# Down projection of a hybrid block: the last convolutions in steps, single PSUM banks for the second block, smaller tiles for the sums of weights

## Chip, cores and metric

The kernel runs on one core of a Trainium2 chip. The metric is the device time of one execution in microseconds; the median of three runs of the kernel before is 1498.23 us (1496.71 to 1498.31). The profile describes one execution, which itself took 1497.91 us. Engines: PE (TensorE, the matmuls), ACT (ScalarE), DVE (VectorE), POOL (GpSimd), SP (SyncE, here only a queue for DMAs).

## The reference

One layer of a transformer block in float32, 256 tokens of width 2048: three kinds of attention with gates, an output projection, and a feed-forward part. The change touches only the last:

```python
h2 = rms_norm(x, g_ffn[l])
u = causal_depthwise_conv(h2 @ w_up[l], conv_w[l], conv_b[l])   # 2048 -> 2 x 5632, three taps along the tokens
u_gate, u_val = jnp.split(u, 2, axis=-1)
x = x + (jax.nn.silu(u_gate) * u_val) @ w_down[l]               # 5632 -> 2048
```

## The kernel before

**Two parts of each number.** Every float32 operand of a matmul is split into a rounded part ("hi", a cast on ACT) and the rest ("lo", a subtraction on DVE), and a product is three matmuls: hi x hi, lo x hi and hi x lo. For the weights, a piece of 128 x 1024 is loaded into a "raw" buffer by SP (four buffers), cast on ACT into one of four hi buffers and subtracted on DVE into one of four lo buffers (`parts`, lines 886 and 887). A hi or lo buffer is free when the matmuls that read it four pieces ago are done.

**Up stage** (lines 791 to 813). The 44 tiles of 128 columns are taken in groups of four, once for the gate half (`s` = 0) and once for the value half (`s` = 1). A group has eight weight pieces and fills two PSUM pairs (a tile of two banks, `two_banks`). After the group `conv` is queued for each pair: it adds the two halves of the product, scales by the norm (`u`), applies three taps (activations on ACT at lines 739 and 743, adds on DVE at 744), and either applies Silu or multiplies by the gate and splits the product into hi and lo in `aT` (lines 750 to 753). `later` queues a generator, `tick` runs one step of each active one (at most `WINDOW` = 2); a `conv` is a generator without a yield, so that one tick issues all of it. Scratch tiles (`cr`, `z`) come from two shared buffers. During the up stage `weight_sums` also loads rows of the down weights into `r` (two buffers of 128 x 2 x 2 x 512) and adds them in place, lines 770 to 773; the sums go to DRAM for the "s" steps below.

**Down stage** (from line 818 on). It has two column blocks of 1024. A block's order is written out in `PLANS`: "e" is a plain product of two tiles of `aT` with two weight pieces, in two steps of 12 matmuls (the last one of a block does nothing in its first step and 24 in its second); "s" is a seven-product scheme in four steps (3, 6, 6 and 6 matmuls), which reads sums of `aT` tiles (`forms`, on DVE and ACT, lines 855 to 867) and the sums of weights. A block has four accumulators X and four Y, a bank each, held in four pair tiles. `gather` adds Y to the residual rows `xr` in three parts, one a tick, beginning three ticks after the last "s"; `finish` runs what is left of it at the block's end, and `results` then adds X (line 1017) and stores (line 1018). The second block begins with X on the pairs that held Y.

**What sets the order.** A list scheduler places the instructions, but `keep_in_program_order` (`keep`, `pin`) puts an instruction behind whatever was traced before it on its engine. All loads, casts and subtractions of the down stage are so pinned. Loads and casts of a step are issued two steps ahead of its matmuls (`AHEAD`). The convolutions of the last group are ticked after the first down step, so in program order they stand behind the casts of three pieces and ahead of the fourth; their own instructions are not pinned. Loads take a raw buffer, from the ninth on every third one a "more" buffer (`buffer`). `down_pool` closes the convolutions' pools and opens its own in their place.

## Time and profile before

| | |
|---|---|
| median of three runs | 1498.23 us |
| profiled execution | 1497.91 us, its span 1496.2 us |
| PE busy | 1482.3 us (99%) |
| DVE busy | 1043.6 us (70%) |
| ACT busy | 862.9 us (58%) |
| DMA | 327.70 MB, mean 219 GB/s |
| mean granted clock of PE | 0.997 |
| PE idle behind other engines, all waits | 7.9 us |
| longest of them | 4.3 us, once |

The span runs from the first to the last instruction. PE's busy time is modelled from the matmuls' starts. The up stage ends and the down stage begins at 1256.3 us, its second block at 1378.1 us, and the last matmul ends at 1490.4 us. Rows of a timeline give start, duration, engine, line, operation, what is written and read, and in brackets the engine's idle time ahead of it and what ended it.

### The profile page before, as it was taken

The numbers are of one execution on the slowest core, as the hardware profiler recorded it, in microseconds if no ns is written. First come the engines' busy times: TensorE is split into PE (matmuls) and PEld (weight loads), VectorE is DVE, ScalarE is ACT, GpSimd is POOL, SyncE is SP. The second block draws the span as 40 slices with busy tenths as digits, with TensorE's granted clock in tenths as the row PEclk, the third lists the DMA queues.
The fourth block names the chain that finished last, engine by engine and source line by source line (L and its number), as shares of the span: only waits on it lengthen the run. The fifth ranks groups of instructions, "written<-read, shape, count | busy, mean of one in ns | idle before, by whom it ended". The sixth has DMA issues, their size and how long they took to land.

```text
span 1496.2 us, 20140 instructions
## 1 busy us (share of the span) xinstructions
PE 1482.3 (99%) x7408; PEld 1250.7 (84%) x7408; DVE 1043.6 (70%) x1333; ACT 862.9 (58%) x1225; POOL 35.8 (2%) x81
## 2 busy tenths in 40 slices
PE   9999999999999999999999999999999998999998
PEld 6888888888888888888888888888888887888886
DVE  5766566555655646556557778778778776998987
ACT  6755454458544444444457667667667666655653
POOL 0000000001000000000000000000000000001000
PEclk9999999999999999999999999999999999999999
DMA  8675475475666677665676877877877774778874
GB/s 296 203 204 157 127 223 157 119 224 149 196 198 206 192 203 199 191 193 191 219 227 221 281 249 257 274 259 241 273 264 248 262 218 151 254 267 257 291 264 155
DMA packets 155921, 327.70 MB, mean 219 GB/s; under 512 B 11290, under 2 KB 20142, under 8 KB 155822
## 3 DMA queue, kind: packets, MB, share of 16 engines
q1 hardware_dynamic: 150798, 310.15, 66.3%
q0 software_dynamic: 4272, 15.21, 2.8%
q8 instruction: 58, 0.95, 0.3%
q10 hardware_dynamic: 752, 1.06, 0.2%
q14 instruction: 41, 0.34, 0.1%
HBM read 312.21 MB, written 14.16 MB: 218 GB/s over the span
## 4 chain that ended last, share of the span: by engine, by line
PE 96%; ACT 2%; DVE 1%; DMA 1%; issue 0%; POOL 0%; SPq 0%; DVEq 0%; POOLq 0%; ACTq 0%
PE u L805 22%; PE u L807 11%; PE g L158 5%; PE g L160 5%; PE g L159 5%; PE d L893 5%; PE d L891 5%; PE d L892 5%; PE s L158 2%; PE s L160 2%; PE f L158 2%; PE f L160 2%; PE s L159 2%; PE f L159 2%; PE b L160 2%; PE b L159 2%
## 5 line engine op out<-in xcount | busy, mean ns | idle before, releaser
L805 PE MATMUL u<-hT,hi_u 128*128 128x512 f32 x1408 | 442.4, 396 | 0.1
L807 PEld LDWEIGHTS u<-hT,lo_u 128*128 128x128 f32 x1408 | 264.5, 188 | 62.5
L807 PE MATMUL u<-hT,lo_u 128*128 128x256 f32 x1408 | 276.6, 278 | 0.0
L148 DVE TENSOR_TENSOR lo_u<-raw_u,hi_u 128x1024 fp32r<-128x1024 f32 x176 | 214.1, 1221 | 72.7 <-ACT hi_u L147 70.9
L147 ACT CAST hi_u<-raw_u 128x1024 fp32r<-128x1024 f32 x176 | 183.4, 1048 | 103.0 <-PE u L805 92.3
L805 PEld LDWEIGHTS u<-hT,hi_u 128*128 128x128 f32 x1408 | 214.4, 189 | 0.5 <-issue 0.5
L148 DVE TENSOR_TENSOR lo_g<-raw_g,hi_g 128x1024 fp32r<-128x1024 f32 x96 | 117.7, 1229 | 101.3 <-ACT hi_g L147 99.0
L147 ACT CAST hi_g<-raw_g 128x1024 fp32r<-128x1024 f32 x96 | 100.8, 1052 | 121.8 <-PE g L159 96.8
L158 PE MATMUL g<-hi_g,xT 128*128 128x512 f32 x384 | 150.9, 393 | 0.0
L160 PE MATMUL g<-lo_g,xT 128*128 128x512 f32 x384 | 149.6, 390 | 0.0
L159 PE MATMUL g<-hi_g,xT 128*128 128x512 f32 x384 | 149.5, 389 | 0.0
L160 PEld LDWEIGHTS g<-lo_g,xT 128*128 128x128 f32 x384 | 72.1, 188 | 15.3
L159 PEld LDWEIGHTS g<-hi_g,xT 128*128 128x128 f32 x384 | 72.2, 188 | 14.6
L158 PEld LDWEIGHTS g<-hi_g,xT 128*128 128x128 f32 x384 | 72.1, 188 | 14.5
L891 PE MATMUL d<-hi_d,aT 128*128 128x512 f32 x200 | 79.0, 395 | 4.3 <-ACT hi_d L886 4.3
L744 DVE TENSOR_TENSOR y<-y,z 128x512 f32<-128x512 f32 x88 | 60.8, 691 | 26.7 <-ACT z L743 22.9
L893 PE MATMUL d<-lo_d,aT 128*128 128x512 f32 x200 | 78.9, 395 | 0.0
L892 PE MATMUL d<-hi_d,aT 128*128 128x512 f32 x200 | 78.8, 394 | 0.0
L743 ACT ACTIVATE z<-u,taps 128x256 f32<-128x256 f32 x176 | 74.6, 496 | 0.0
L148 DVE TENSOR_TENSOR lo_s<-raw_s,hi_s 128x1024 fp32r<-128x1024 f32 (+1 forms) x40 | 44.7, 1118 | 37.2 <-ACT hi_s L147 37.1
L148 DVE TENSOR_TENSOR lo_f<-raw_f,hi_f 128x1024 fp32r<-128x1024 f32 (+1 forms) x40 | 44.7, 1120 | 34.5 <-ACT hi_f L147 33.0
L147 ACT CAST hi_f<-raw_f 128x1024 fp32r<-128x1024 f32 (+1 forms) x40 | 38.6, 967 | 52.3 <-PE f L159 47.6
(324 smaller groups left out, 2796.6 us busy)
## 6 DMA issues: line engine op xcount, KB each, us to landing
raw_u<-in_w_up_dram SPq DMA_DIRECT2D x176, 512.0 KB, 4.7
raw_g<-in_w_in_dram SPq DMA_DIRECT2D x96, 512.0 KB, 3.8
raw_d<-in_w_down_dram SPq DMA_DIRECT2D x50, 512.0 KB, 5.4
r<-in_w_down_dram SPq DMA_DIRECT2D x76, 256.0 KB, 5.6
raw_s<-in_w_down_dram SPq DMA_DIRECT2D x38, 512.0 KB, 5.2
raw_f<-in_w_in_dram SPq DMA_DIRECT2D x32, 512.0 KB, 3.6
raw_s<-in_w_in_dram SPq DMA_DIRECT2D x32, 512.0 KB, 3.6
raw_o<-in_w_out_dram SPq DMA_DIRECT2D x32, 512.0 KB, 5.0
```

Of the source, the lines that this page charges most:

```text
L147: pin(nc.scalar.copy(hi[:, :m], raw[:, :m]))
L148: pin(nc.vector.tensor_tensor(lo[:, :m], raw[:, :m], hi[:, :m].bitcast(F32), ALU.subtract))
L158: nc.tensor.matmul(o, lhsT=xh, rhs=wh, start=first, stop=False)
L159: nc.tensor.matmul(o, lhsT=xl, rhs=wh, start=False, stop=False)
L160: nc.tensor.matmul(o, lhsT=xh, rhs=wl, start=False, stop=last)
L743: nc.scalar.activation(z[:, i], u[:, i, j : j + S], AF.Copy, scale=taps_of(j, i))
L744: nc.vector.tensor_tensor(y, y, z, ALU.add)
L805: nc.tensor.matmul(ps, lhsT=hi[:, j, c], rhs=hT[:, k + j, :], start=first, stop=False)
L807: nc.tensor.matmul(ps[:, :S], lhsT=lo[:, j, c], rhs=hT[:, k + j, :S], start=False, stop=last)
L891: nc.tensor.matmul(o, lhsT=ah, rhs=w[0], start=first, stop=False)
L892: nc.tensor.matmul(o, lhsT=al, rhs=w[0], start=False, stop=False)
L893: nc.tensor.matmul(o, lhsT=ah, rhs=w[1], start=False, stop=last)
```

## The change

- `conv` of the last group's value half (`tail`: tiles 40 and 42) yields five times, so that it takes six ticks: scaled product; first two activations with the middle tap; last tap; product with the gate; hi part; lo part. There are now two `u` tiles that take turns. `tick` lets four generators be active in the down stage.
- `PLANS`: the first block has five "e" before its first "s" and two after its last "s" (before: four and three). Its forms begin with the fourth "e" instead of the second. "More" buffers are used from the twelfth load on.
- The second block's accumulators are eight single-bank tiles of a new pool, opened when the pair pool closes. The list of tiles is turned by half, as the list of pairs was.
- `weight_sums` has the first row's halves in a tile `r0` with one buffer and the second row's in `r1` with two. The sums and their order are the same.

```diff
-PLANS = ("eeee" + "se" * 8 + "ee", "e" + "se" * 4 + "sse" + "se" * 3 + "ssee")
+PLANS = ("eeeee" + "se" * 7 + "see", "e" + "se" * 4 + "sse" + "se" * 3 + "ssee")
...
-    waiting, active = deque(), []
+    waiting, active, window = deque(), [], [WINDOW]
...
-        while waiting and len(active) < WINDOW:
+        while waiting and len(active) < window[0]:
...
-    pp2.append(ctx.enter_context(tc.tile_pool(name="pp2", bufs=4, space=bass.MemoryType.PSUM, reuse_waits="tile")))
+    pp2x = ctx.enter_context(ExitStack())
+    pp2.append(pp2x.enter_context(tc.tile_pool(name="pp2", bufs=4, space=bass.MemoryType.PSUM, reuse_waits="tile")))
...
-        u = cp.tile([P, 2, S + 2], F32, tag="u", bufs=1, name="u")
-        nc.vector.memset(u[:, :, 0:2], 0.0)
-        cps.extend((cp, u, sp))
+        us = [cp.tile([P, 2, S + 2], F32, bufs=1, name=f"u{i}") for i in range(2)]
+        for u in us:
+            nc.vector.memset(u[:, :, 0:2], 0.0)
+        cps.extend((cp, us, sp))
...
     def conv(ps, f, s):
-        cp, u, _ = cps
+        cp, us, _ = cps
+        u = us[f // 2 % 2]
...
+        tail = f >= FT - 4 and s == 1
...
         nc.vector.tensor_tensor(u[:, :, 2:], cr, rbc.unsqueeze(1).to_broadcast([P, 2, S]), ALU.mult)
+        if tail:
+            yield
...
             nc.vector.tensor_tensor(y, y, z, ALU.add)
+            if tail:
+                yield
...
             nc.vector.tensor_tensor(g, g, y, ALU.mult)
+            if tail:
+                yield
             a = aT[:, f : f + 2]
             nc.scalar.copy(a[:, :, :S], g)
+            if tail:
+                yield
             nc.vector.tensor_tensor(a[:, :, S:], g, a[:, :, :S].bitcast(F32), ALU.subtract)
-        return
-        yield
-
+            ended.append(f)
...
-        r = cps[2].tile([P, 2, 2, 512], F32, tag="r", name=f"r_{nb}_{p}")
+        r = [
+            cps[2].tile([P, 2, 512], F32, tag=f"r{j}", bufs=1 + j, name=f"r{j}_{nb}_{p}") for j in range(2)
+        ]
         for j, n in ((0, 1), (0, 0), (1, 1), (1, 0)):
             tc.keep_in_program_order(
-                nc.sync.dma_start(r[:, j, n], dv[:, 2 * p + j, n0 + n * 512 : n0 + (n + 1) * 512])
+                nc.sync.dma_start(r[j][:, n], dv[:, 2 * p + j, n0 + n * 512 : n0 + (n + 1) * 512])
             )
...
-        b01 = r[:, 0, 1]
-        tc.keep_in_program_order(nc.vector.tensor_tensor(r[:, 0, 0], r[:, 0, 0], b01, ALU.add))
+        add = lambda o, i: tc.keep_in_program_order(nc.vector.tensor_tensor(o, o, i, ALU.add))
+        add(r[0][:, 0], r[0][:, 1])
         yield 1
-        tc.keep_in_program_order(nc.vector.tensor_tensor(r[:, 1, 1], r[:, 1, 1], r[:, 0, 0], ALU.add))
-        tc.keep_in_program_order(nc.vector.tensor_tensor(r[:, 1, 0], r[:, 1, 0], r[:, 1, 1], ALU.add))
+        add(r[1][:, 1], r[0][:, 0])
+        add(r[1][:, 0], r[1][:, 1])
...
-        if turn[0] > 8 and turn[0] % 3 == 0:
+        if turn[0] > 10 and turn[0] % 3 == 0:
...
     def start(nb):
-        b = [two_banks(f"d{nb}_{i}") for i in range(4)]
-        if nb:
-            b = b[2:] + b[:2]
-        X = [[b[t][:, n] for n in range(2)] for t in range(NT)]
-        Y = [b[2 + i // 2][:, i % 2] for i in range(4)]
-        banks[nb] = X, Y
+        if nb == 0:
+            pairs = [two_banks(f"d{nb}_{i}") for i in range(4)]
+            b = [pair[:, i] for pair in pairs for i in range(2)]
+        else:
+            pp2x.close()
+            pp3 = ctx.enter_context(tc.tile_pool(name="pp3", bufs=8, space=bass.MemoryType.PSUM, reuse_waits="tile"))
+            b = [pp3.tile([P, 512], F32, tag="bank", name=f"d{nb}_{i}") for i in range(8)]
+            b = b[4:] + b[:4]
+        banks[nb] = [[b[2 * t + n] for n in range(2)] for t in range(NT)], b[4:]
...
-                if formed < ns and n_done >= 2:
+                if formed < ns and n_done >= 4 - 2 * nb:
...
+    window[0] = 4
     for f in after_step.pop(-1):
         f()
```

More of the change, by code (lines that the diff above doesn't have):

```diff
@@ L750, in conv @@
             nc.vector.tensor_tensor(g, g, y, ALU.mult)
+            if tail:
+                yield
             a = aT[:, f : f + 2]
             nc.scalar.copy(a[:, :, :S], g)
+            if tail:
+                yield
             nc.vector.tensor_tensor(a[:, :, S:], g, a[:, :, :S].bitcast(F32), ALU.subtract)
-        return
-        yield
+            ended.append(f)
+    ended = []
     made = {}
@@ L776, in weight_sums @@
         yield 2
-        nc.gpsimd.dma_start(T, r[:, 1].rearrange("p b n -> p (b n)"))
+        nc.gpsimd.dma_start(T, r[1].rearrange("p b n -> p (b n)"))
     adding = []
@@ L821, in down_pool @@
         if not dn:
+            assert len(cps) == 3 and len(ended) == FT // 2
             uv.close()
```

## The prediction

> **What bounds the kernel now.** The page's first part comes first: TensorE (PE) is busy for the whole span, so only time in which PE stands still or runs slowly can be won. The answer on PE's waits lists that time. Line 891 is the first matmul of a product in the down stage, and its one wait of 4.3 us is more than all others together.

> ```profile
> span 1496.2 us, 20140 instructions
> PE 1482.3 (99%) x7408; PEld 1250.7 (84%) x7408; DVE 1043.6 (70%) x1333; ACT 862.9 (58%) x1225; POOL 35.8 (2%) x81
> ...
> PE d L891 <- ACT hi_d L886: 4.3, 1, 4.3
> PE spare L102 <- DVE qscale L244: 1.2, 1, 1.2
> PE mT L195 <- DMA memres<-in_mem_dram: 1.2, 1, 1.2
> ```

> Next, the timeline of PE around that wait, and the sums by stretch (their columns: length, busy time of PE, PEld, DVE, ACT, POOL, then the granted clock, DMA share, GB/s).

> ```profile
> 1263.98 0.39 PE L892 MATMUL d<-hi_d,aT 128*128 128x512 f32 x1
> 1264.21 0.39 PE L893 MATMUL d<-lo_d,aT 128*128 128x512 f32 x1
> 1268.89 0.79 PE L891 MATMUL d<-hi_d,aT 128*128 128x512 f32 x1 [4.29 <-ACT hi_d L886]
> ...
> 1274.58 0.47 PE L891 MATMUL d<-hi_d,aT 128*128 128x512 f32 x1
> 1274.89 0.39 PE L892 MATMUL d<-hi_d,aT 128*128 128x512 f32 x1
> ...
> 1264.40:1268.90 4.50, 0.21 (x2) 0.01 (x1) 2.80 (x5) 3.02 (x7) 1.64 (x3) 0.89 0.27 95
> 1268.90:1274.60 5.70, 5.66 (x13) 3.97 (x14) 5.37 (x9) 3.57 (x6) 0.00 (x0) 0.50 0.71 213
> 1300.00:1320.00 20.00, 20.00 (x90) 16.57 (x89) 19.80 (x31) 12.74 (x16) 0.00 (x0) 1.00 0.75 260
> ```

> Matmuls normally start 0.227 us apart, so the one at 1268.89 was due at 1264.44: 4.45 us lost. After the pause the granted clock is 0.50 for 5.7 us. From 1268.89 to 1274.89 lie 13 starts, 6.00 us where 13 x 0.227 = 2.95 would do: 3.05 more. The stall is worth **7.5 us**, not 4.3.

> Its cause stands on ACT's timeline.

> ```profile
> 1253.45 1.05 ACT L886 CAST hi_d<-raw_d 128x1024 fp32r<-128x1024 f32 x1 [1.74 <-PE u L805]
> 1255.77 0.59 ACT L734 COPY cr<-u 128x512 f32<-128x512 f32 x1 [1.27 <-PE u L807]
> 1257.84 1.10 ACT L739 ACTIVATE y<-u,taps 128x256 f32<-128x256 f32 x2 [1.48 <-DVE u L736]
> 1258.84 1.70 ACT L743 ACTIVATE z<-u,taps 128x256 f32<-128x256 f32 x4
> 1260.55 0.59 ACT L734 COPY cr<-u 128x512 f32<-128x512 f32 x1
> 1262.49 0.62 ACT L752 CAST aT<-y 128x512 fp32r<-128x512 f32 x1 [1.36 <-DVE y L750]
> ...
> 1267.27 0.62 ACT L752 CAST aT<-y 128x512 fp32r<-128x512 f32 x1 [1.49 <-DVE y L750]
> 1267.80 2.94 ACT L886 CAST hi_d<-raw_d 128x1024 fp32r<-128x1024 f32 x3
> ```

> Three casts of down weights are done by 1254.5. Then come both last convolutions, one after the other, 12 us of which ACT spends 4.3 waiting for DVE; the fourth cast is pinned behind them and starts at 1267.80. PE has three steps of 12 x 0.227 = 2.72 us in hand from 1256.27 and runs dry at 1264.44.

> **The last convolutions in six steps.** No instruction is added; what each of the steps 0 to 5 puts ahead of the next cast changes. I walk the queues with the durations of the rows. ACT: both copies end at 1257.1, the fourth cast at 1258.1 (it needs the last up matmul's buffer, free at 1256.3). Then two activations and two scalings of each convolution, 2 x 1.9, to 1261.9; fifth cast to 1262.9; the other scalings, 2 x 0.85, to 1264.6; sixth cast to 1265.6. DVE: four operations of about 0.65 to 1259.1, the low part of the fourth piece to 1260.3; two adds, fifth low part to 1264.1; two adds, sixth to 1266.8; products, seventh to 1269.2. PE wants pieces four to seven at 1264.44, 1267.16, 1269.88 and 1272.60: each is 3 us early or more. Over the ten first steps (27.2 us, five "e" now) DVE has nine low parts (1.15 each), 12 operations of the convolutions (0.65) and two sets of forms (2.8): 23.8 us. So the stall goes, and with it the half clock: **-7.5**, with -4.45 as the poorer bound if some other short wait still costs the clock. The second u buffer is what lets the two convolutions overlap; earlier it changes nothing, since the two scratch buffers keep them in turn.

> **Plan and forms.** The matmuls are the same (8 "s" and 14 "e" in the first block). Forms start two "e" later, so six "se" pairs carry one instead of five. The row of 1300 to 1320 is such a stretch: DVE 19.80 of 20.00 us, and PE never waits. I cost it at 0; what hides it is PE's lead over DVE, and without that one more set of forms is 2.8 us late. Load nine goes to a raw buffer instead of a "more" one: it can start when piece five is read out, at 1264.1, 13.9 us before its step (1256.27 + 8 x 2.72): 0.

> **Sums of weights.** The first half now has one buffer, so its next load, which is on SP's queue, waits for the add at line 772 of the sum before, and the up weights queue behind it.

> ```profile
> 1175.51 0.42 SPq L765 DMA_DIRECT2D r<-in_w_down_dram  x1
> 1176.82 0.37 SPq L146 DMA_DIRECT2D raw_u<-in_w_up_dram  x1
> ...
> 1180.22 0.69 DVE L772 TENSOR_TENSOR r<-r 128x512 f32<-128x512 f32 x1
> ...
> 1183.83 1.05 ACT L147 CAST hi_u<-raw_u 128x1024 fp32r<-128x1024 f32 x1 [1.73 <-PE u L805]
> ...
> DMA to landing us min/median/max: 3.6/4.7/6.6
> ```

> The load slips from 1175.51 to 1180.91 and the up piece from 1176.82 to 1181.35. It lands 6.6 us later at worst (the last row, of raw_u), at 1188.0; cast 1.05 and low part 1.23 end at 1190.3. That piece is second in its group; the group's copies on ACT come each 22.29 us, PE needs it at 1256.27 - 3 x 22.29 + 2.79 = 1192.2. Cost **0**, with 1.9 us to spare.

> **Single banks at the end.** The DVE rows are the last sums of the first and the second block.

> ```profile
> 1378.26 1.29 DVE L1017 TENSOR_TENSOR xr<-xr,d 128x512 f32<-128x512 f32 x2 [1.35 <-PE d L893]
> ...
> 1487.74 1.28 DVE L1017 TENSOR_TENSOR xr<-xr,d 128x512 f32<-128x512 f32 x2
> 1490.46 1.35 DVE L1017 TENSOR_TENSOR xr<-xr,d 128x512 f32<-128x512 f32 x3 [1.43 <-PE d L893]
> 1488.46 4.05 ACTq L1018 DMA_DIRECT2D out_dram<-xr  x5
> GB/s 0 0 0 0 0 46 337 391 364 373 355 319 146 0 0 0 0 55 346 373 387 314 332 323 196 5 0 0 0 0 0 0 0 0 36 0 0 0 0 0
> ```

> The last row is the DMA rate in 40 slices from 1488 to 1497. The third sum has its matmuls complete 1.36 us (six matmuls) before the last, but waits for the whole pair; so three adds and three stores follow the last matmul. With banks of their own only two halves follow: the last store is issued at 1490.46 + 0.41 + 0.03 + 0.47 = 1491.4 instead of 1492.0. I take **-0.65**; the bounds are 0, if the stores are slow for another reason, and -1.35, if the 256 KB that no longer share the end also bring the landing forward (0.7 us at 373 GB/s).

> **Single banks at the boundary of the blocks.** Here the change can take back. Before, the second block's X (which its first step writes) takes the pairs that held Y. The new pool is a fresh one, and the reordering of the list by the code doesn't choose places: in the compiled kernel before, a fresh pool gives place 0 to the tile used first, then places from the top down (the pair pool: banks 0, 6, 4, 2). X of the first block lies in banks 0-1 and 6-7. The new X then gets 0, 7, 6 and 5: the second matmul triple of the block waits for the last of the four result adds. When is that? Only two "e" follow the last "s" now, so parts two and three of the gathering of Y come together in the last step.

> ```profile
> 1369.39 0.68 DVE L990 TENSOR_TENSOR f<-e,d 128x512 f32<-128x512 f32 x1
> 1371.31 1.22 DVE L887 TENSOR_TENSOR lo_d<-raw_d,hi_d 128x1024 fp32r<-128x1024 f32 x1
> 1372.44 0.68 DVE L994 TENSOR_TENSOR xr<-xr,e 128x512 f32<-128x512 f32 x1
> 1374.49 1.22 DVE L887 TENSOR_TENSOR lo_d<-raw_d,hi_d 128x1024 fp32r<-128x1024 f32 x1
> ...
> 1372.60 1.05 ACT L886 CAST hi_d<-raw_d 128x1024 fp32r<-128x1024 f32 x1 [1.66 <-PE d L892]
> ...
> 1378.06 0.39 PE L891 MATMUL d<-hi_d,aT 128*128 128x512 f32 x1
> 1378.74 0.39 PE L891 MATMUL d<-hi_d,aT 128*128 128x512 f32 x1
> ```

> In the old clock times: the cast ends at 1373.65, its low part at 1374.9; gathering 1.92 + 2.05 (the distances 1369.39 to 1371.31 and 1372.44 to 1374.49) to 1378.8; four adds to 1381.3. PE wants the first triple at 1378.06 (its adds end at 1380.1) and the second at 1378.74: it stands 2.05 us, runs 0.68, stands 0.55, and is **+2.6** late. Bounds: 0, if X gets Y's old banks (those are read out at 1378.2, before the third triple's turn at 1379.42), and 2.6 + 3.05 if the clock drops too. Behind the waiting matmul stands all of PE; the casts behind it only gain lead.

> On whether 2.05 us lowers the clock there is a row from the start:

> ```profile
> 12.63 0.44 PE L195 MATMUL mT<-ident,memres 128*128 128x128 f32 x2 [1.17 <-DMA memres<-in_mem_dram]
> ...
> 12.00:14.00 2.00, 1.37 (x7) 1.19 (x8) 1.83 (x3) 1.38 (x3) 0.00 (x0) 1.00 0.73 268
> ```

> 1.17 us of idling left 1.00, 4.29 us gave 0.50; 2.05 is nearer the first. [...]

> **Sum**, against the profiled execution (1497.91 us, span 1496.2): -7.5 - 0.65 + 2.6 = -5.55, a span of 1490.65. The median of the runs is 0.32 above the profiled one; from 1498.23 the forecast is **1492.7**.

> **Rivals.**
> 1. The boundary costs nothing (X lands on Y's old banks, or the scheduler finds other matmuls): -8.15, **1490.1**. For it: before, no wait stands at the boundary. Against it: the order of places.
> 2. The boundary's pauses lower the clock: +3.05, **1495.7**. Against it stands the 1.17 us row; for it, two pauses close together.
> 3. The change doesn't do what it says: the convolutions' pieces are not themselves pinned, and if they still stand in one run ahead of the fourth cast, the 7.5 us stay: **1500.2**. Against it: every cast is pinned behind whatever was traced before it.
> 4. Slower by SP: the single buffer of the sums. The place is the second piece of 18 groups; it decides from a landing of 8.5 us (6.6 + 1.9), and each further 0.5 us costs 18 x 0.5 = 9: **1501.7**. Against it: 6.6 is the slowest landing seen.

> **How the numbers follow.** Forecast 0.50, rival 1 0.27, rival 2 0.10, rival 3 0.07, rival 4 0.03, anything else (the extra forms' 2.8 us, 1495.5, among it) 0.03. The range must hold the forecast, rival 1 with its end at the better bound (1490.1 - 0.7 = 1489.4) and rival 2 (1495.7): 1489.4 to 1496.0. A measurement of this kernel tells about 0.2% (3 us) from no change, so faster means under 1495.2: forecast, rival 1 and a third of rival 2, 0.80; same 0.10; slower 0.10.

> **What would show it.** Right: no wait of line 891 on the casts near 1264, granted clock 1.00 there; the copies of line 734 both ahead of the fourth cast, the scalings after it; a PE wait on the sums of line 1017 near 1371 (1378 less 7.5), about 2.6 us in all with the clock at 1.00; after the last matmul two adds and two stores. Wrong: that wait absent (rival 1), a clock under 1 behind it (rival 2), PE waits on up casts (rival 4), or any wait of PE on low parts between steps 10 and 40, which would mean that DVE could not carry the moved forms.

## The result, and the profile after

The changed kernel takes **1492.72 us** (median of six runs, 1491.44 to 1494.12). The kernel before, in six runs beside it, takes 1498.06 us (1496.71 to 1498.36). The ratio is 0.9964, with a 95% interval of 0.9954 to 0.9974: faster, by about 0.36%. The profiled execution is the slowest of the six, 1494.12 us.

Page of the changed kernel, first part:

```profile
span 1492.4 us, 20170 instructions
...
PE 1483.2 (99%) x7408; PEld 1252.3 (84%) x7408; DVE 1043.4 (70%) x1334; ACT 862.4 (58%) x1225; POOL 35.6 (2%) x81
```

PE's waits in the changed kernel (total, times, longest). Line 906 is the first matmul of a product (891 before), line 1035 the addition of the results (1017 before):

```profile
PE d L906 <- DVE xr L1035: 2.2, 2, 2.0
PE spare L102 <- DVE qscale L244: 1.2, 1, 1.2
```

The wait of 4.3 us on a cast is gone. A new one has come, twice, 2.2 us in all, on the results of the first block.

**Where the stall went.** ACT's timeline in the changed kernel, from the last casts of the up stage on (start, duration, instruction):

```profile
1254.45 1.05 ACT L901 CAST hi_d<-raw_d 128x1024 fp32r<-128x1024 f32 x1 [1.74 <-PE u L819]
1256.77 1.28 ACT L738 COPY cr<-u 128x512 f32<-128x512 f32 x2 [1.27 <-PE u L821]
1257.95 1.05 ACT L901 CAST hi_d<-raw_d 128x1024 fp32r<-128x1024 f32 x1
1259.41 1.10 ACT L745 ACTIVATE y<-u,taps 128x256 f32<-128x256 f32 x2 [0.41 <-DVE u L740]
...
1263.00 1.03 ACT L901 CAST hi_d<-raw_d 128x1024 fp32r<-128x1024 f32 x1
1263.94 1.70 ACT L749 ACTIVATE z<-u,taps 128x256 f32<-128x256 f32 x4
1265.55 1.98 ACT L901 CAST hi_d<-raw_d 128x1024 fp32r<-128x1024 f32 x2
```

Both copies now stand together and the fourth cast right behind them, at 1257.95 where it was at 1267.80. The convolutions' scalings fill the gaps between the casts. (In this execution the down stage begins 1.0 us later than in the one before, at 1257.27; so 1.0 us is to be taken off when times are set side by side.)

**Where the new wait is.** PE at the boundary of the two blocks, and below it DVE over the same time:

```profile
1371.29 0.39 PE L908 MATMUL d<-lo_d,aT 128*128 128x512 f32 x1
1373.67 0.47 PE L906 MATMUL d<-hi_d,aT 128*128 128x512 f32 x1 [1.99 <-DVE xr L1035]
...
1374.20 0.40 PE L908 MATMUL d<-lo_d,aT 128*128 128x512 f32 x1
1374.77 0.79 PE L906 MATMUL d<-hi_d,aT 128*128 128x512 f32 x1 [0.17 <-DVE xr L1035]
...
1378.30 0.40 PE L908 MATMUL d<-lo_d,aT 128*128 128x512 f32 x1
...
1371.63 0.69 DVE L1011 TENSOR_TENSOR xr<-xr,e 128x512 f32<-128x512 f32 x1
1372.24 2.47 DVE L1035 TENSOR_TENSOR xr<-xr,d 128x512 f32<-128x512 f32 x4
```

The four result additions end at 1374.71. The first triple of the second block starts at 1373.67 instead of 1371.52 (the start before it plus 0.227), and the second at 1374.77, right behind the fourth addition.

The sums by stretch of the changed kernel (length, busy time of PE, PEld, DVE, ACT, POOL, then granted clock, DMA share, GB/s):

```profile
1373.30:1374.80 1.50, 0.96 (x4) 0.52 (x4) 1.50 (x4) 0.00 (x0) 1.40 (x3) 1.00 0.33 126
1374.80:1376.50 1.70, 1.70 (x4) 1.42 (x5) 1.70 (x3) 0.00 (x0) 0.92 (x3) 0.50 0.91 313
1376.50:1378.30 1.80, 1.80 (x6) 1.38 (x6) 1.16 (x2) 0.00 (x0) 0.94 (x3) 0.52 0.85 228
1378.30:1380.00 1.70, 1.70 (x9) 1.41 (x8) 0.42 (x1) 1.05 (x1) 0.66 (x2) 1.00 1.27 128
1257.30:1285.00 27.70, 27.70 (x125) 22.93 (x124) 24.92 (x38) 18.48 (x31) 0.00 (x0) 1.00 0.63 203
```

The last row is the place of the old stall: PE busy for all of it, at full clock. The rows above it show that in this execution the new pauses are followed by 3.5 us at half clock. From 1374.77 to 1378.30 lie eight starts, 3.53 us where 8 x 0.227 = 1.82 would do: 1.7 us more.

**The end.** DVE's last additions and the issues of the stores in the changed kernel:

```profile
1486.86 0.69 DVE L1035 TENSOR_TENSOR xr<-xr,d 128x512 f32<-128x512 f32 x1 [0.23 <-PE d L908]
1488.22 0.75 DVE L1035 TENSOR_TENSOR xr<-xr,d 128x256 f32<-128x256 f32 x2 [0.67 <-PE d L908]
...
1486.07 3.43 ACTq L1036 DMA_DIRECT2D out_dram<-xr  x5
```

The third sum no longer waits for the last matmul (it starts at 1486.86, the matmuls end at 1488.18). Only two halves follow, and the last store is issued 0.87 us behind the last matmul, where it was 1.62 before.

The three stretches, from the traces: the down stage from its first matmul's start to its last one's end, and from there to the end of the span.

| | down stage | from its end to the span's end |
|---|---|---|
| before | 234.16 | 5.75 |
| changed | 230.91 | 4.23 |
| difference | -3.25 | -1.52 |

The sum is -4.8; the two profiled spans differ by 3.8, since this execution reached the down stage 1.0 us later.

### The profile page after: what moved, and what is told of

It is laid out like the page before. It is cut to its first block, busy times and chain, and to the rows that moved or that the text cites. A ratio compares the mean times of both kernels' runs of the same rounds, so it can differ in the third digit from the quotient of the medians.

```text
span 1492.4 us, 20170 instructions
## 1 busy us (share of the span) xinstructions
PE 1483.2 (99%) x7408; PEld 1252.3 (84%) x7408; DVE 1043.4 (70%) x1334; ACT 862.4 (58%) x1225; POOL 35.6 (2%) x81
## 3 DMA queue, kind: packets, MB, share of 16 engines
q0 software_dynamic: 4272, 15.21, 2.8%
## 5 line engine op out<-in xcount | busy, mean ns | idle before, releaser
L147 ACT CAST hi_u<-raw_u 128x1024 fp32r<-128x1024 f32 x176 | 182.8, 1048 | 109.8 <-PE u L819 78.4
L147 ACT CAST hi_g<-raw_g 128x1024 fp32r<-128x1024 f32 x96 | 100.8, 1052 | 121.8 <-PE g L159 97.2
L750 DVE TENSOR_TENSOR y<-y,z 128x512 f32<-128x512 f32 x88 | 60.6, 690 | 21.2 <-ACT z L749 17.6
L147 ACT CAST hi_f<-raw_f 128x1024 fp32r<-128x1024 f32 (+1 forms) x40 | 38.6, 967 | 52.5 <-PE f L159 47.6
```

What stands on the lines that cost most here:

```text
L147: pin(nc.scalar.copy(hi[:, :m], raw[:, :m]))
L750: nc.vector.tensor_tensor(y, y, z, ALU.add)
```

## Experiments

**Theory**: the change is three separate sums. The convolutions in steps win the whole stall, pause and half clock, about 7.5 us. The boundary gives back 2.7 us, since the fresh pool puts the second block's X on the banks that are read out last. The end wins somewhat more than a microsecond. **Rivals**: the boundary's wait comes from the later gathering (the moved "e"), whatever bank X has; the stall was won by the second u buffer, the moved "e" or the smaller sums, not by the steps; and the boundary's price is mostly the half clock, not the pauses.

| kernel | edit | median us (range, runs) | ratio to before (95%) |
|---|---|---|---|
| e0_again | the changed kernel | 1493.14 (1491.86 to 1493.96, 6) | 0.9969 (0.9956 to 0.9981) |
| e1_placed | X on the banks of the old Y | 1488.65 (1488.55 to 1489.80, 5) | 0.9941 (0.9928 to 0.9953) |
| e2_whole | last convolutions in one step | 1498.95 (1498.28 to 1501.51, 10) | 1.0011 (1.0002 to 1.0020) |
| e3_pairs | second block in pairs again | 1490.24 (1489.87 to 1491.04, 5) | 0.9950 (0.9938 to 0.9963) |
| e4_plan | plan of before | 1490.11 (1489.87 to 1491.18, 5) | 0.9951 (0.9938 to 0.9963) |
| e5_sums_only | before, with the smaller sums alone | 1498.06 (1496.81 to 1499.95, 11) | 1.0001 (0.9992 to 1.0010) |
| e6_long | two more additions ahead of the results | 1494.71 (1493.83 to 1495.73, 11) | 0.9980 (0.9971 to 0.9989) |
| e7_banks_only | before, with the single banks (and the smaller sums) | 1497.63 (1496.56 to 1499.16, 11) | 1.0001 (0.9992 to 1.0009) |

The first four ran beside a median of 1497.90 us for the kernel before, the others beside 1497.83. All but e6_long compute what the kernel computes in the same additions and products; e6_long adds two additions whose results nothing uses.

### e0_again: the same kernel once more

> The changed kernel once more, unaltered. Its profile showed two PE waits on the result adds at the block boundary (1.99 and 0.17 us) and then half clock for 3.5 us; its six times spread over 2.7 us. Theory: the waits are in every execution (about 2.5 us late), the half clock only in some, so that a profile near 1491.5 us shows the same waits with the clock at 1.00, and one near 1494 us shows half clock. Rival: the spread comes from elsewhere (the start of the program), and the half clock is there whatever the time. Median 1492.7 by both.

Measured 1493.14 us. Waits and stretches of this profile:

```profile
PE d L906 <- DVE xr L1035: 2.2, 2, 2.0
PE kv L158 <- ACT memT L183: 1.9, 1, 1.9
```

```profile
0.00:10.00 10.00, 6.87 (x22) 3.93 (x23) 2.67 (x7) 3.26 (x5) 1.50 (x10) 0.91 0.70 237
10.00:20.00 10.00, 10.00 (x50) 8.44 (x49) 6.03 (x9) 5.36 (x9) 0.00 (x0) 0.92 0.74 246
1374.90:1378.50 3.60, 3.43 (x16) 2.81 (x16) 3.26 (x6) 1.05 (x1) 2.04 (x4) 1.00 0.89 282
```

The boundary has the same two pauses, 1.99 and 0.17 us, and this time the clock behind them stays at 1.00 (16 matmuls in 3.60 us). So the half clock is no fixed part of the boundary's price: it came in one profiled execution and not in the other. Here another pause, 1.9 us near the start of the program, lowered the clock instead (0.91 and 0.92 over the first 20 us); so this execution took 1492.90 us and not the 1491.5 expected of one with a clock of 1.00 at the boundary. Of the twelve executions of this kernel (six here, six in the section on the result) eight have a mean clock of 0.998 over the whole run, three 0.999 and one 1.000; of the fifteen of e1_placed, e3_pairs and e4_plan none has 0.998 and thirteen have 1.000. A half clock somewhere is thus common in this kernel; how often it stands at the boundary, two traces can't tell.

### e1_placed: where X lies

```diff
-            pp3 = ctx.enter_context(tc.tile_pool(name="pp3", bufs=8, ...))
-            b = [pp3.tile([P, 512], F32, tag="bank", name=f"d{nb}_{i}") for i in range(8)]
-            b = b[4:] + b[:4]
+            pools = [
+                ctx.enter_context(tc.tile_pool(name=n, bufs=c, ...))
+                for n, c in (("pa", 2), ("px", 4), ("pb", 2))
+            ]
+            own = [pools[i].tile([P, 512], F32, tag="bank", ...) for k, i in enumerate((1, 1, 1, 1, 0, 0, 2, 2))]
+            b = own
```

Three pools in place of one are meant to put X on banks 2 to 5, which held Y, and Y on 0, 1, 6 and 7. No profile names the banks; what it can show is whether the waits go.

> The changed kernel with the second block's accumulators in three pools of 2, 4 and 2 banks, so that X lies on the banks that held Y, and Y on those that held X. Theory (the boundary wait is a matter of places): no PE wait on the result adds, no half clock there, 2.5 us less in every execution and some 1.7 us less in those with half clock: median 1489.3 us (1488.8 to 1490.2). Rival (DVE is simply late at the boundary, and the wait moves to the next casts or to Y): PE waits 1 to 2.5 us somewhere between the boundary and 10 us later, median 1491.5 to 1492.7.

Measured 1488.65 us, better than both kernels. All waits of PE in this profile, and the stretch around the boundary:

```profile
PE mT L195 <- DMA memres<-in_mem_dram: 1.5, 2, 1.0
PE spare L102 <- DVE qscale L244: 1.2, 1, 1.2
PE r L613 <- POOL sb L590: 0.2, 1, 0.2
```

```profile
1366.00:1374.00 8.00, 8.00 (x37) 6.63 (x36) 7.89 (x12) 2.68 (x3) 1.83 (x4) 1.00 0.57 206
```

DVE is as late as in the changed kernel (7.89 of 8.00 us busy, and the four additions start at 1371.03, 114.98 us into the down stage, where the changed kernel has 114.97), but PE does not wait for it. The down stage is 226.61 us long, one matmul each 0.227 us throughout: no wait is left in it. e0_again's down stage, with the clock at 1.00, is 229.32: the place of X costs **2.71 us**. The rival that the late gathering costs it by itself falls. The medians differ by 4.5, more than the 2.7. The traces show two other parts: 1.7 us of half clock behind the boundary where it occurs, and the part of the program ahead of the down stage, which begins at 1256.05 here and at 1257.27 and 1257.61 in the two traces of the changed kernel. How much of the 4.5 each of them has in the medians is not shown.

### e2_whole: are the steps the cause?

```diff
-        tail = f >= FT - 4 and s == 1
+        tail = False
```

> The changed kernel with the last two convolutions issued whole in one tick, all else as changed. Theory (the steps between the casts remove the stall): line 906 waits about 4.3 us for the fourth cast, half clock follows, 7.5 us more than the changed kernel: 1500.2 us, less if DVE's two convolutions overlap better with two u tiles (the run of convolutions could shorten by up to 2 us, then 1496 to 1500). Rival (the later forms, the fifth plain product ahead and the larger window do it): no stall, 1492.7 us.

Measured 1498.95 us, 5.8 more than e0_again, and no faster than before. Waits of PE:

```profile
PE d L906 <- ACT hi_d L901: 4.3, 1, 4.3
PE d L906 <- DVE xr L1035: 2.2, 2, 2.0
```

The old wait is back in full, with the second u buffer, the moved "e" and the single banks still there; so the rest of the change doesn't remove it without the steps. The steps in turn need neither the single banks (e3_pairs) nor the moved "e" (e4_plan), which have them and no such wait; whether they need the second u buffer, the later forms and the four active generators, no run tells. The down stage is 236.38 us, 7.06 more than e0_again's. The ten times fall in two groups, six at 1498.3 to 1499.0 and four at 1500.6 to 1501.5. The four have a mean clock of 0.996, the six 0.997 or 0.998. The 2 us between the groups are near the 1.7 that a half clock at the boundary cost, but only one of the ten was traced, one of the six (mean clock 0.997): its boundary has the same two waits, 2.2 us in all, the longest 2.0. That a half clock there parts the two groups is not shown.

### e3_pairs: pairs for the second block

The edit puts the body of `start` of the kernel before back (four pair tiles, the list turned by two).

> The changed kernel with the second block's accumulators in pairs, as before, all else as changed. Theory: X lies on the pairs of Y, so no PE wait at the boundary; at the end three adds and three stores follow the last matmul again. Against the kernel with placed single banks it is slower by the end's gain alone: 1.5 us if the changed profile's end (4.2 us from the last matmul to the end of the span against 5.8 before) is the gain, so 1490.8 us; 0.65 us by the prediction's term, so 1490.0. Rival (single banks cost nothing at the boundary): 1492.7 plus the end, 1493.4 to 1494.2 us.

Measured 1490.24 us: 2.9 less than e0_again and 1.59 more than e1_placed. PE has no wait at the boundary, and the down stage is 226.61 us as with e1_placed. What is lost lies at the end, DVE and store issues:

```profile
1481.27 1.28 DVE L1032 TENSOR_TENSOR xr<-xr,d 128x512 f32<-128x512 f32 x2
1483.99 1.35 DVE L1032 TENSOR_TENSOR xr<-xr,d 128x512 f32<-128x512 f32 x3 [1.43 <-PE d L908]
...
1481.99 4.05 ACTq L1033 DMA_DIRECT2D out_dram<-xr  x5
```

Three additions behind the last matmul, as before, and 5.38 us from the matmul to the end of the span where e1_placed has 4.24. The single banks win **1.15 us** at the end. In this kernel they cost more at the boundary than they win.

### e4_plan: the plan of before

```diff
-PLANS = ("eeeee" + "se" * 7 + "see", ...)
+PLANS = ("eeee" + "se" * 8 + "ee", ...)
```

> The changed kernel with the first block's old order of plain and seven-product steps (four plain ones ahead, three behind the last seven-product step); the forms still begin with the fourth plain one. Theory (the boundary wait is the last result add against the second triple; the gathering of Y in the last step makes it late): three plain ones behind let the gathering end earlier, only the two adds that need the last matmuls remain, so one PE wait of 0.9 us instead of 2.0 and 0.2 (2.5 us late in all), and no half clock: about 1.7 us less than the changed kernel without half clock, median 1490.9 us (1490.2 to 1491.5). Rival (the plan was moved because DVE cannot carry the forms so early): PE waits on low parts around the first seven-product steps, 1493 us or more.

Measured 1490.11 us, just under the expected 1490.2 to 1491.5. The boundary in this profile, PE and DVE:

```profile
1371.02 0.39 PE L908 MATMUL d<-lo_d,aT 128*128 128x512 f32 x1
1372.11 0.50 PE L906 MATMUL d<-hi_d,aT 128*128 128x512 f32 x1 [0.70 <-DVE xr L1035]
...
1370.77 1.28 DVE L1035 TENSOR_TENSOR xr<-xr,d 128x512 f32<-128x512 f32 x2 [1.36 <-PE d L908]
```

And the stretch behind it:

```profile
1373.10:1376.60 3.50, 3.50 (x17) 2.86 (x16) 3.12 (x4) 1.05 (x1) 1.74 (x4) 1.00 0.93 208
```

With one more "e" behind the last "s" the gathering is over sooner, and DVE even waits 1.36 us for the last pair of X to be complete. What remains is one pause, with the clock at 1.00 behind it, after which PE is 1.0 us late in all (the down stage's 226.61 becomes 227.61). So of the 2.7 us at the boundary 1.7 come from the moved "e", and 1.0 stays with the old plan too while X lies on these banks. The plan itself won nothing that shows: no wait for a low part appears without it.

### e5_sums_only: the smaller sums by themselves

The edit takes `weight_sums` of the change into the kernel before, and nothing else.

> The kernel before with the smaller tiles for the sums of weights alone (the first row's tile with one buffer). Theory: the load of a sum and the up piece behind it slip by about 5 us on SP's queue, PE never notices: no PE wait in the up stage, 1498.0 us, within 0.1% of before. Rival (the slip reaches PE in some of the 18 groups): PE waits on casts of up weights, each 0.5 us in 18 groups would be 9 us, 1507.

Measured 1498.06 us, ratio 1.0001 (0.9992 to 1.0010). PE's only wait in the down stage is the old one, `PE d L893 <- ACT hi_d L888: 4.3, 1, 4.3`. The smaller sums cost nothing and win nothing; they make room for the second u buffer.

### e6_long: a longer pause

```diff
+        if nb == 0:
+            for _ in range(2):
+                keep(tt(e, e, e, ALU.add))
```

These two additions stand behind the gathering of the first block and ahead of the result additions.

> The changed kernel with two more additions on DVE (128x512, results not used) behind the gathering of the first block, so that the result adds end 1.4 us later. Theory (the half clock follows a pause of more than about 3 us always, one of 2 us by chance): PE waits 3.4 and 0.2 us, the clock is at half for some 3.5 to 6 us in every execution: 1.4 us plus 1.7 to 3 us more than the changed kernel without half clock (about 1491.9): 1495 to 1496.5 us. Rival (the half clock comes by chance whatever the pause): 1.4 us more, 1494.5 us.

Measured 1494.71 us, 1.6 more than e0_again: just under the theory's 1495 to 1496.5, and nearer to the rival's 1494.5. The rival added its 1.4 us to a median that has half clocks in it already, so the time alone doesn't part the two. Waits, and the stretches behind the pause:

```profile
PE d L906 <- DVE xr L1038: 3.4, 1, 3.4
```

```profile
1374.50:1378.00 3.50, 3.46 (x9) 2.35 (x8) 3.46 (x5) 0.00 (x0) 2.02 (x5) 0.52 0.86 300
1378.00:1380.00 2.00, 2.00 (x10) 1.62 (x10) 0.34 (x1) 1.05 (x1) 0.88 (x2) 0.99 1.01 123
```

The pause is 3.44 us, and over the 3.5 us behind it the clock is 0.52. The theory's border of about 3 us is shown by no run: pauses of 1.99 us gave 0.50 (changed kernel) and 1.00 (e0_again), and none between 1.99 and 3.44 us was traced. The down stage is 232.14 us, 5.53 more than e1_placed's. The two additions put the result additions back by 1.4 us (they start 2.06 us after the start of the gathering's last addition, in e1_placed 0.61). If only that counted, the kernel would take 1488.65 + 2.71 + 1.4 = 1492.8; it takes 1.9 more, and its lowest time, 1493.83, is still above that. None of the eleven has a mean clock above 0.999. So a pause of this length probably met the half clock in all or nearly all of its executions, though only one of them is traced. The changed kernel's own pauses met it in one of two traced executions: the boundary's price is 2.7 us for the pauses, and 1.7 more in some executions.

### e7_banks_only: the single banks without the steps

The edit takes `start` of the change (and `weight_sums`, which e5_sums_only puts at zero) into the kernel before.

> The kernel before with single banks for the second block alone. Theory: the last convolutions' stall stays (4.3 us); at the boundary one PE wait of about 0.9 us on the result adds appears (the gathering is done early by the old plan); the end is 1.15 to 1.5 us shorter: 1497.6 us, 0.2 to 0.7 us less than before. Rival (the boundary wait is as in the changed kernel): 2.5 us more and 1.3 less, 1499.2 us.

Measured 1497.63 us, ratio 1.0001 (0.9992 to 1.0009). Waits of PE:

```profile
PE d L892 <- ACT hi_d L887: 4.3, 1, 4.3
...
PE d L892 <- DVE xr L1021: 0.7, 1, 0.7
```

The pause of e4_plan at the boundary is there (0.70, PE 0.97 us late), and the end is 4.58 us instead of 5.75, so 1.17 shorter. The two nearly cancel, and the time says "no difference" of a change that does two things. (In this trace the first block is also 0.60 us shorter than in the kernel before.)

## Why the prediction was right

Forecast 1492.7 us, measured 1492.72. It was right in direction, in the mechanism of the tail and in that of the boundary's waits; it was not right about the clock behind them in the profiled execution, and the end was mis-sized. That the last tenths agree is luck, as the points on rival 2 and on the end show.

**The tail, -7.5.** It holds. Before, the down stage was 234.16 us, in e1_placed it is 226.61: 7.55 less. The order on ACT and DVE came as walked: fourth cast behind the two copies, then scalings and casts in turn. No wait of PE is left there and the clock is 1.00; e2_whole shows that without the steps the rest of the change doesn't do it. The poorer bound of -4.45 was not met. The stall's price is no constant: e2_whole, with the same wait of 4.3 us, pays 7.06 for it.

**The boundary, +2.6.** It holds: 2.71 between e0_again and e1_placed, by the mechanism named. The walk had the last result addition at 1381.3 in the old clock times, which is 1374.8 in this trace (less 7.5, plus 1.0); it ended at 1374.71. The pauses were forecast as 2.05 and 0.55 and are 1.99 and 0.17 (what the profile calls idle is less than the lateness). e1_placed then showed that rival 1's mechanism, X on the banks of the old Y, is to be had, and what it gives: 1488.65, against 1490.1 worked out.

**Rival 2, the half clock behind the boundary** (1495.7, given one chance in ten), is the point where I chose a single outcome for what happens at times. The profile of the changed kernel shows it and that of e0_again doesn't. The row of 1.17 us could not decide it, and I took the pause to be nearer to that than to 4.29. The step that fails here is to go by the length of the pause: the same pauses gave both outcomes, and what parts them is how they lie in the clock's windows (last section). The expected time should have carried part of it: it is worth 1.7 us where it occurs, not the 3.05 of the rival. The mark named for the forecast, a clock of 1.00 behind the pause, thus failed in one of two traces.

**The end, -0.65, was mis-sized.** Measured: 1.15 (e3_pairs against e1_placed), 1.52 between the traces before and after. Its issue part was nearly right: the last store is issued 0.75 us sooner. What I took for a bound only, that the last store also lands sooner, came about (that the fewer bytes beside it are the cause is argued, not shown). The landing times of the stores, first before (line 1018), then in the changed kernel (line 1036):

```profile
DMA to landing us min/median/max: 2.6/3.6/4.1
```

```profile
DMA to landing us min/median/max: 2.2/3.1/4.3
```

The last store, the shortest of each, lands in 2.58 us before and in 2.16 after: 0.42 more. Together that is 1.17, as e7_banks_only has it. The further 0.35 between the two first traces lies behind the landing (1.55 us there, 1.20 here); e5_sums_only has 1.20 with the old stores and e7_banks_only 1.56 with the new ones, so it is no effect of the change.

These two errors offset each other. By the measured terms the sum without a half clock is -7.55 - 1.17 + 2.71 = -6.01, which from 1498.06 gives 1492.05; the median stands 0.7 above that, and the fastest execution, 1491.44, had a mean clock of 1.000 where the slowest, 1494.12, had 0.998. That the 0.7 is the half clock's share is argued from these numbers, not shown; the start of the program, after which the down stage began 1.0 us later in the profiled execution than in the kernel before, is another candidate.

**Sums, 0.** Right in price, wrong in a detail. SP's issues in the changed kernel, with the addition that frees the buffer and the cast of the up piece:

```profile
1182.10 1.30 SPq L779 DMA_DIRECT2D r<-in_w_down_dram  x3
1183.51 0.38 SPq L146 DMA_DIRECT2D raw_u<-in_w_up_dram  x1
...
1181.39 0.68 DVE L783 TENSOR_TENSOR r<-r,r 128x512 f32<-128x512 f32 x1
...
1184.83 1.05 ACT L147 CAST hi_u<-raw_u 128x1024 fp32r<-128x1024 f32 x1 [1.73 <-PE u L819]
```

The load of the sums does wait for the addition (which ends at 1182.07; the load is issued at 1182.10), as I said. But the up piece of the walk doesn't queue behind it: its cast is at 1184.83, that is 1183.83 plus the 1.0 us of this execution. Up loads are not pinned, and here they stand ahead of the sum's loads on the queue. One later piece, issued at 1183.51, does follow three of them; its cast starts at 1191.34, 1.0 us later than before (1189.37) when the 1.0 us of this execution is taken off, and waits 0.87 us for the load. PE waits for neither, so rival 4's point of decision was not reached.

**Plan and forms, 0.** Right for the forms: no wait of PE for low parts appears. But the plan was costed there as free, while its price stood in the boundary's term; e4_plan shows that 1.7 of the 2.7 us are the plan's.

**Rival 3** (the steps do nothing) fell with the first timeline.

## What to carry to other kernels

The price of the long wait here was what PE was late plus what the clock took afterwards: 4.3 us of wait were worth 7.5 (7.06 in e2_whole). So the last pieces of a stage should be spread between the first casts of the next one. When accumulators get a fresh pool, look up where the tiles land and give the first ones used the banks that are read out first; here that one choice nearly doubled the gain (1488.65 against 1493.14 us, from 1497.90). An edit that makes no difference may be two that cancel, as the single banks alone did (-1.17 and +0.97); the trace by stage tells them apart, the time does not.

## What the runs showed of the hardware that was not expected

| trace | window | PE busy in it | clock in the next |
|---|---|---|---|
| kernel before | 1264.49 to 1267.90 | 0.11 us | 0.50 |
| e6_long | 1371.21 to 1374.62 | 0.65 us | 0.50 |
| changed kernel | 1371.40 to 1374.81 | 1.25 us | 0.50 |
| e0_again | 4.81 to 8.22 | 1.48 us | 0.50 |
| e0_again | 1370.14 to 1373.56 | 1.88 us | 1.00 |
| kernel before | 11.80 to 15.21 | 2.58 us | 1.00 |

In the traces before and after the change, from the start of the clock's record on, every window at full clock with PE busy for 1.25 us or less is followed by half clock (0.11 and 1.25 in the table, 0.65 and 0.73 in the windows in which the matmuls of the program end); the least busy of all the rest is the one of 2.58 us in the table. The pause of 1.99 us fell into one window in the changed kernel and was split between two in e0_again. As to the return, windows at half clock with PE busy for 3.41 us (changed kernel) and 3.37 (e6_long) brought 1.00 back, one of 2.39 (the kernel before, 1267.90 to 1271.32) did not. The busy times count modelled ends of matmuls, and where between 1.48 and 1.88 us the border lies is not shown.

At the very start a granted clock of 1.00 is no evidence: in the changed kernel the clock's record begins at 12.89 us, and matmuls ahead of it (7.80, 8.22, 8.65, 9.08) start 0.43 us apart as they do at half clock (1376.20, 1376.63, 1377.06), in rows that say 1.00. In the kernel before it begins at 4.97 us, ahead of the pause of 1.17 us.

**The last store landed sooner where less went out beside it**: 2.16 instead of 2.58 us from issue to landing at the same size, when the 256 KB that went out with it before had left earlier. The last two stores, 128 KB each, have a median of 2.2 us in e0_again too, as in the changed kernel, and of 2.6 before. That the other store is the cause is argued, not shown.
